# Two of the three modulation groups of each layer: issued beside the input projection, or beside the grouped-query attention

## The chip, the cores and the metric

The kernel runs on one core of one Trainium2 chip. The metric is the device time of one execution in microseconds; lower is better. Runs of one kernel scatter: the three shown below lie between 3043.15 and 3050.22 us.

## The reference

Two layers of a diffusion trunk work on 1024 sample tokens and 128 prompt tokens of width 1024. What matters here is the modulation (adaLN): two conditioning vectors, one for the sample tokens and one for the prompt tokens, go through a matrix of 1024 x 6144 in each layer, and the six rows of 1024 numbers that come out shift, scale and gate the layer's two halves.

```python
def _modulation(cvec, w, b):
    m = (jax.nn.silu(cvec) @ w + b)[:, None, :]
    return jnp.split(m, 6, axis=-1)

def _layer(x, mod, lw, ctx):
    ...
    sh1, sc1, g1, sh2, sc2, g2 = mod
    h = _rms(x, n1) * (1 + sc1) + sh1
    ...
    u_conv, qa, ka, va, qn, kn, vn = jnp.split(h @ w_in, idx, axis=-1)
    a_out = _conv_module(u_conv, dw_w, dw_b, ln_g, ln_b)
    ...
    x = x + g1 * (jnp.concatenate([a_out, b_out, c_out], axis=-1) @ w_out)
    h = _rms(x, n2) * (1 + sc2) + sh2
    x = x + g2 * (jnp.square(jax.nn.relu(h @ w1)) @ w2)
```

Here `b_out` is the grouped-query attention (6 query heads, 2 key heads, 1152 keys for a sample token) and `c_out` the neighbourhood attention. Shift and scale of the first half (`sh1`, `sc1`) are needed ahead of the projection `h @ w_in`; the other four not before the output projection `@ w_out`.

## The kernel before

The activation lies transposed in SBUF. Each layer runs through these stages: modulation group 0, first norm, convolution input, input projection, grouped-query attention, neighbourhood attention, output projection, second norm, MLP. All run on one core, and the engines' instruction streams are in program order: generators are advanced by hand, one piece at a time, and the order of these calls is the order of the instructions on every queue. A tile framework adds the semaphores.

**Modulation** (`modulation`, L183). The 6144 columns are cut into three groups of 2048: group 0 is `sh1` and `sc1`, group 1 is `g1` and `sh2`, group 2 is `sc2` and `g2`. One group runs over eight k-steps. A k-step takes four weight tiles `aw` (128 x 512, 256 KB each) and multiplies each with the two vectors `silc` into the PSUM tile `psmod` (four matmuls in the program, L224, eight records in the trace), and then issues the four DMAs for the next k-step's tiles on the SyncE queue (helper line L144). Ahead of the k-steps stands a DVE memset of `psmod` (L219); behind them a DVE copy to `mt` (L229), four transposes on TensorE into `psmt` (L233), and small DVE operations that write `mod` and one of the factors `A`. Groups 1 and 2 of a layer form one generator, `fill`. It has 23 steps: one that only fetches, and for each group a memset, eight k-steps, the copy, and the transposes with what follows them.

**Input projection** (`project`, L689). Seven column chunks (A0 to A5, then VN) by five token groups (four of two 128-token tiles, one of one tile). A token group is 24 matmuls per tile into `pst` (L541 to L543: the high and the low half of the fp32 operands in three products); then `post` takes the statistics of the heads (ACT `sq`, DVE `ss` L420), normalises (DVE `nt`, `y`, `xn`), turns the positions or applies a gain on GpSimd (L471, L484 to L490), and stores `o` to scratch in DRAM (`ddA`, `dvA`). Once per token group the convolution takes one step: DVE taps `cacc` (L102) and GpSimd taps `cacc` (L570, fed by ACT). Weights come in as `wr` and are split into `wh` (ACT) and `wl` (DVE). After every second token group (`g % 2 == 0`, three of five) the projection advances `fill` by one step: 21 of the 23 steps of a layer happen here.

**Keys.** While the last chunk VN still runs, the attention is begun: SyncE loads the keys `kd` back from `ddA`, and TensorE transposes them (`pstr` L784). This load waits for the stores of the chunks ahead of it.

**Grouped-query attention** (`gqa`, L1001, driven by `attention`, L1251). Six units of nine key tiles, with two yields per key tile, 108 ticks in all. Scores go to `psst` (L1132, L1133), the row maxima of the next unit to `psm` (L1044) and then over DVE (`mx` L1046, `nmx`) and TensorE (`psnm` L1035) into the queries, the exponentials through ACT, the products with the values to `psacc` (L1118), and the row sums through GpSimd and DVE adds `R` and TensorE (`pssum` L1084). Convolution's tail runs beside it. At each tick `attention` calls `next(fill, None)`: before the change only the last two steps of `fill` are left for it.

`aw`, `mt` and many other short-lived tiles share one ring of 18 SBUF buffers (tag T); `psmod`, `psmt`, `pst`, `psst` and the rest share eight PSUM banks.

Of the kernel before, what the change touches and what calls it, by code (L numbers as in the profile page):

```python
# [45 lines left out]
def hybrid_step(ctx, tc, I, O, depth=DEPTH):  # L46
# [104 lines left out]
    def flush(every=False):  # L151
        for x in stores:
            x[0] -= 1
        while stores and (every or stores[0][0] <= 0):
            _, out, in_ = stores.pop(0)
            load(out, in_)
# [163 lines left out]
    def run(g):  # L320
        for _ in g:
            pass
# [169 lines left out]
    def post(L, c, t, nt, ps):  # L492

        x = ps[:, 0:nt * 256].rearrange("p (t c) -> p t c", t=nt)
        o = T([nt, 256], n="o")
        lo, hi = slice(0, 128), slice(128, 256)
        normed = {"A2": hi, "A5": lo, "VN": None}.get(c, slice(0, 256))
        if normed is not None:
            st = head_stats(x[:, :, normed], nt)
        rest = {"A2": lo, "A5": hi, "VN": slice(0, 256)}.get(c)  # L500
        if rest is not None:
            acopy(o[:, :, rest], x[:, :, rest])
        yield
        if normed is not None:
            xn = head_norm(*st)
            if c in ("A0", "A1"):
                post_rope(L, c, t, nt, xn, o)
            else:
                gain(o[:, :, normed], xn, 2 if c in ("A2", "A3") else 3, nt, L)
        if t == 8:  # L510
            l, p = L.l, o[:, 0, :]
            for d, k, a, b, e in (("A1", "new_attn_k", 0, 128, 128), ("A2", "new_attn_v", 0, 0, 128), ("A4", "new_na_k", 0, 0, 256),
                                  ("A5", "new_na_k", 256, 0, 128), ("A5", "new_na_v", 0, 128, 128), ("VN", "new_na_v", 128, 0, 256)):
                if c == d:
                    store(O[k][l][:, a:a + e], p[:, b:b + e])
        if normed is not None:
            for u in range(nt):
                for d in range(2):
                    store(L.dd[c][:, t + u, :].rearrange("p (h d x) -> p h d x", d=2, x=64)[:, :, d, :],
                          o[:, u, normed].rearrange("p (h x) -> p h x", x=64))  # L520
        if rest is not None:
            store(L.dv[c][:, t:t + nt, :], o[:, :, rest])
        yield
# [10 lines left out]
    def tok_group(L, t, nt, w):  # L534
        ps = P("pst")
        for u in range(nt):
            o = ps[:, u * 256:(u + 1) * 256]
            for k in range(KT):
                hi, lo = stat(L, t + u, k)
                wh, wl = w[k]  # L540
                mm(o, hi, wh, start=(k == 0), stop=False)  # L541
                mm(o, hi, wl, start=False, stop=False)  # L542
                mm(o, lo, wh, start=False, stop=(k == KT - 1))  # L543
        return ps
# [144 lines left out]
    def project(L, pr, pre, fill):  # L689

        conv = conv_in(L, pr, pre, fill)
        next(conv)
        w = pr.weights("A0")
        for c in ORDER[2:]:
            for g, (t, nt) in enumerate(GROUPS):
                ps = tok_group(L, t, nt, w)
                if g in (1, 3):
                    pr.step()
                two = post(L, c, t, nt, ps)
                next(two)  # L700
                if conv is not None:
                    if next(conv, 0) == 0:
                        conv = None
                        L.conv = conv_all(L)
                else:
                    next(L.conv, None)
                next(two)
                if g % 2 == 0:
                    next(fill, None)
                flush()  # L710
                if c in ("A5", "VN"):
                    yield c
            if c != "VN":
                w = pr.weights(ORDER[ORDER.index(c) + 1])
            if c == "A1":
                L.tabs = None
        L.h = None
        flush(True)


    def conv_all(L):
        yield from conv_taps(L)
        l = L.l
        L.cin = None
        for si, o, n in OFFS:
            m = n // 128
            ps = P("psmu")
            for j in range(2):
                mm(ps[:, 0:n], ones, L.acc[j][:, o:o + n], start=(j == 0), stop=(j == 1))
            yield  # L730
            sqs = []
            for j in range(2):
                a = L.acc[j][:, o:o + n]
                stt(a, ps[:, 0:n], -1.0 / 256.0, a, ALU.mult, ALU.add)
                sq = T([n], n="lsq")
                act(sq, a, ACTF.Square)
                sqs.append(sq)
            yield
            tt(sqs[0], sqs[0], sqs[1], ALU.add)
            yield  # L740
            pv = P("psvr")
            mm(pv[:, 0:n], ones, sqs[0], start=True, stop=True)
            y = T([n], n="lrs")
            rsq_start(pv[:, 0:n], y, 256)
            yield
            rsq_end(pv[:, 0:n], y, sqs[1], 256)
            yield
            for j in range(2):
                a = L.acc[j][:, o:o + n]
                tt(a, a, y, ALU.mult)  # L750
            yield
            for j in range(2):
                a = L.acc[j][:, o:o + n]
                act(a, a, ACTF.Identity, scale=cvec(l, 1, j), bias=cvec(l, 2, j))
                yield
                sg = T([n], n="lsg")
                ts(sg, a, -1.0, ALU.mult, 44.0, ALU.min)
                yield
                sigmoid_end(sg)
                yield  # L760
                tt(a, a, sg, ALU.mult)
            yield

    def conv_out(L):

        yield from L.conv
        for si, o, n in OFFS:
            for j in range(2):
                a = L.acc[j][:, o:o + n]
                for chi, clo, c in c_put(si, j, 0, n):  # L770
                    acopy(chi, a[:, c])
                    yield
                    tt(clo, a[:, c], f32(chi), ALU.subtract)
                    yield
        L.acc = None
# [475 lines left out]
    def attention(L, proj, fill, op, out):  # L1251

        g = gqa(L)
        c = next(proj)
        while c:
            for _ in range(STEPS[c]):
                if L.unit < 0:
                    next(g)
            c = next(proj, None)
        while L.unit < 0:  # L1260
            next(g)
        tail = conv_out(L)
        n = natten(L)
        for i, _ in enumerate(g):
            if i % 2:
                next(tail, None)
            next(fill, None)
            if L.unit == 5 and (not L.prepared or i in (6 * 18 - 5, 6 * 18 - 2)):
                next(n)
        run(tail)  # L1270
        k = 0
        for _ in n:
            next(L.pend, None)
            next(fill, None)
            if L.step == 24:
                op.begin()
            if L.step > 25:
                for _ in range(2):
                    next(out)
        run(L.pend)  # L1280
# [513 lines left out]
    with tc.manual_schedule():  # L1794
# [4 lines left out]
        fill = modulation(0, [1, 2])  # L1799
        for l in range(depth):  # L1800
            last = l == depth - 1
            op, M = OutProj(L), Mlp(l)
            out = out_proj(L, op, M)
            attention(L, project(L, pr, pre, fill), fill, op, out)
            run(fill)
            while next(out) == "begun":
# [69 lines left out]
            fill = modulation(l + 1, [1, 2])  # L1876
# [89 lines left out]
```

## Time and profile before

| | us |
|---|---|
| median of 3 runs | 3045.22 |
| lowest, highest | 3043.15, 3050.22 |
| the profiled execution's own time | 3043.87 |
| its span in the trace | 3042.1 |
| TensorE busy over the span | 2857.0 (94%) |
| VectorE busy | 2082.6 (68%) |
| ScalarE busy | 1404.7 (46%) |
| GpSimd busy | 655.7 (22%) |
| mean granted TensorE clock | 0.97 |

The span is what the trace covers; 1.8 us of the execution lie around it. The shares are means over stages with quite different limits, so they say little of a single one. Two stages matter here, once per layer. In layer 0 the projection's first chunk starts at about 122 us and the last score maxima ahead of the attention proper end at about 348 us; the six units of the attention follow, up to about 540 us. In layer 1 the same stages begin about 1500 us later. The first k-step of `fill` in layer 0 starts at 138.9 us, and the last at 340.3 us.

### The profile page before, as it was taken

To read this page: it belongs to the slowest core of one execution; us is meant where nothing else is said; L and a number is where in the kernel's file an instruction comes from. 1 tells how busy PE (TensorE), PEld (TensorE's weight loads), DVE (VectorE), ACT (ScalarE), POOL (GpSimd) and SP (SyncE) were. 2 spreads that over 40 slices of the span, in tenths; PEclk is the share of its full clock that TensorE was granted. 3 is DMA by queue.
4 is the path that set the end of the run, shared out by engine and by line. 5 is a ranking of instruction groups with operands and counts; after the bars stand their busy time and mean duration, and the time that the engine had idled before them with its cause. 6 is when DMAs were issued, how large, how long until landed. Compare 5 with 4: busy or idle time off the path is not lost.

```text
span 3042.1 us, 52749 instructions
## 1 busy us (share of the span) xinstructions
PE 2857.0 (94%) x20328; PEld 2538.6 (83%) x20328; DVE 2082.6 (68%) x3985; ACT 1404.7 (46%) x2880; POOL 655.7 (22%) x607
## 2 busy tenths in 40 slices
PE   6998999999799998999889999999997999899999
PEld 3788645899799998999878885458997999899998
DVE  6587777855767555758665877878457765575676
ACT  4334366753544443433452353668345444334343
POOL 3576346310000000000225762553000000000000
PEclk7999999999899998999999999999998999999999
DMA  7376202433366557443433771033334653565334
GB/s 280 91 198 182 85 24 54 109 90 112 132 196 209 195 167 290 146 153 94 138 130 90 189 215 42 17 95 87 98 103 158 202 184 128 192 228 174 125 94 164
DMA packets 424124, 430.42 MB, mean 141 GB/s; under 512 B 120000, under 2 KB 299968, under 8 KB 423872
## 3 DMA queue, kind: packets, MB, share of 16 engines
q1 hardware_dynamic: 423872, 427.04, 45.1%
q8 instruction: 160, 2.62, 0.4%
q14 instruction: 92, 0.75, 0.1%
HBM read 298.50 MB, written 128.45 MB: 140 GB/s over the span
## 4 chain that ended last, share of the span: by engine, by line
PE 71%; DVE 15%; DMA 4%; ACT 4%; issue 2%; POOL 2%; SPq 1%; DVEq 0%; ACTq 0%; POOLq 0%
PE ps L1319 21%; PE psa L1319 7%; PE psc L1319 6%; PE pso L1319 5%; PE psb L1319 5%; PE psacc L1118 3%; DVE cacc L102 2%; PE pspv L985 2%; PE pspt L969 2%; PE pst L541 2%; PE pst L542 2%; PE pst L543 2%; PE psst L1132 2%; PE psd L1319 2%; PE psm L1044 2%
## 5 line engine op out<-in xcount | busy, mean ns | idle before, releaser
L1319 PE MATMUL ps<-ts,w2h 128*128 128x288 f32 x3584 | 635.9, 299 | 42.7 <-ACT w2h L96 29.1
L1319 PEld LDWEIGHTS ps<-ts,w2h 128*128 128x128 f32 x3584 | 534.3, 191 | 48.7 <-ACT w2h L96 37.2
L1319 PE MATMUL ps<-ts,w2l 128*128 128x288 f32 x1792 | 387.5, 298 | 2.0 <-DVE w2l L99 2.0
L96 ACT CAST ts<-ti 128x576 fp32r<-128x576 f32 x256 | 172.0, 672 | 328.2 <-PE ps L1319 209.1
L541 PE MATMUL pst<-wh,HA 128*128 128x256 f32 x1040 | 297.7, 286 | 0.0
L542 PE MATMUL pst<-wl,HA 128*128 128x256 f32 x1040 | 294.4, 283 | 0.1
L1319 PEld LDWEIGHTS ps<-ts,w2l 128*128 128x128 f32 x1792 | 292.2, 191 | 2.4 <-DVE w2l L99 2.2
L543 PE MATMUL pst<-wh,HA 128*128 128x256 f32 x1040 | 293.3, 282 | 0.0
L93 ACT ACTIVATE ev<-ev 128x576 f32<-128x576 f32 x224 | 153.7, 686 | 279.1 <-DVE ev L99 275.6
L99 DVE TENSOR_TENSOR ts<-ti,ts 128x576 fp32r<-128x576 f32 x256 | 195.2, 762 | 68.0 <-ACT ts L96 68.0
L102 DVE SCALAR_TENSOR_TENSOR X<-ps,mod,X 128x288 f32<-128x288 f32 x336 | 112.1, 409 | 173.5 <-PE ps L1319 173.5
L541 PEld LDWEIGHTS pst<-wh,HA 128*128 128x128 f32 x1040 | 198.1, 191 | 19.2 <-issue 6.9
L99 POOL TENSOR_TENSOR nacc<-nacc,nsq 128x512 f32<-128x512 f32 (+1 forms) x12 | 18.9, 1577 | 848.7 <-ACT nsq L93 848.7
L542 PEld LDWEIGHTS pst<-wl,HA 128*128 128x128 f32 x1040 | 198.2, 191 | 0.4 <-DVE wl L99 0.3
L543 PEld LDWEIGHTS pst<-wh,HA 128*128 128x128 f32 x1040 | 198.2, 191 | 0.0
L1755 POOL COPY yu<-X 128x128 f32<-128x128 f32 x8 | 3.9, 500 | 872.6 <-DVE X L102 872.6
L99 DVE TENSOR_TENSOR w1l<-w1r,w1h 128x512 fp32r<-128x512 f32 x128 | 87.9, 690 | 137.1 <-ACT w1h L96 136.8
L1319 PE MATMUL pso<-HA,woh 128*128 128x288 f32 x1024 | 177.8, 295 | 0.0
L1046 DVE TENSOR_REDUCE mx<-psm 128x1 f32<-128x384 f32 x288 | 142.1, 547 | 29.5 <-PE psm L1044 29.3
L1319 PE MATMUL psa<-HA,w1h 128*128 128x288 f32 x768 | 141.0, 307 | 22.0 <-ACT w1h L96 22.0
L93 ACT ACTIVATE pt<-psst 128x512 f32<-128x512 f32 x216 | 118.1, 597 | 87.7 <-PE psst L1133 86.9
L99 POOL TENSOR_TENSOR R<-R,pt 128x1024 f32<-128x1024 f32 x60 | 149.3, 2489 | 24.4 <-ACT pt L93 22.4
(275 smaller groups left out, 7065.5 us busy)
## 6 DMA issues: line engine op xcount, KB each, us to landing
ti<-hd SPq DMA_DIRECT2D x128, 576.0 KB, 3.9
hd<-ev SPq DMA_DIRECT2D x224, 288.0 KB, 3.8
aw<-in_ada_w SPq DMA_DIRECT2D x160, 256.0 KB, 3.8
w1r<-in_mlp_w SPq DMA_DIRECT2D x160, 256.0 KB, 4.4
HF<-in_mlp_w SPq DMA_DIRECT2D x128, 256.0 KB, 5.0
ddA<-o SPq DMA_DIRECT2D x144, 128.0 KB, 2.9
wr<-in_w_in SPq DMA_DIRECT2D x28, 512.0 KB, 4.0
qd<-ddA SPq DMA_DIRECT2D x48, 256.0 KB, 3.3
```

The source lines that it names most:

```text
L93: nc.scalar.activation(out=out, in_=in_, func=func, scale=scale, bias=bias, **k)
L96: nc.scalar.copy(out, in_)
L99: (eng or nc.vector).tensor_tensor(out=out, in0=a, in1=b, op=op)
L102: nc.vector.scalar_tensor_tensor(out=out, in0=a, scalar=s, in1=b, op0=op0, op1=op1)
L541: mm(o, hi, wh, start=(k == 0), stop=False)
L542: mm(o, hi, wl, start=False, stop=False)
L543: mm(o, lo, wh, start=False, stop=(k == KT - 1))
L969: nc.tensor.transpose(ps[0:n, c], self.p[j][:, o:o + n], ident)
L985: mm(ps[64 * j:64 * j + 64, 0:128], v[j], self.at[j, i], start=(i == 0), stop=(i == nb - 1))
L1046: nc.vector.tensor_reduce(out=mx[j][:, qt, b:b + 1], in_=ps[:, 0:384], op=ALU.max, axis=AX.X)
L1118: mm(acc[64 * j:64 * j + 64, :], v, pt[:, j, :], start=(kt == 0), stop=(kt == 8))
L1319: mm(ps[h][:, 0:HH], x, y[:, h * HH:(h + 1) * HH], start=(start and z == 0), stop=(stop and z == 2), skip_group_check=True)
```

## The change

Two lines go out of `project`, and the call in `attention` is made in one tick out of four:

```diff
--- before.py
+++ after.py
@@ -705,8 +705,6 @@
                 else:
                     next(L.conv, None)
                 next(two)
-                if g % 2 == 0:
-                    next(fill, None)
                 flush()
                 if c in ("A5", "VN"):
                     yield c
@@ -1264,7 +1262,8 @@
         for i, _ in enumerate(g):
             if i % 2:
                 next(tail, None)
-            next(fill, None)
+            if i % 4 == 2:
+                next(fill, None)
             if L.unit == 5 and (not L.prepared or i in (6 * 18 - 5, 6 * 18 - 2)):
                 next(n)
         run(tail)
```

All 23 steps now stand in the attention: the fetch at tick 2, the first memset at tick 6, k-steps at ticks 10 to 38, the copy at 42, transposes at 46, and so on for the second group up to tick 90. `fill` has 27 chances in 108 ticks, so it ends there.

The instruction order shows it at three places. First TensorE in the middle of the projection of layer 0, before the change; `wh` and `wl` are weight halves, `HA` halves of the normed activation:

```order
L541 MATMUL pst_1259<-wh_767,HA_74 128x256
L542 MATMUL pst_1259<-wl_768,HA_74 128x256
L543 MATMUL pst_1259<-wh_767,HA_82 128x256
L224 MATMUL psmod_1171<-aw_1010,silc 2x512
L224 MATMUL psmod_1171<-aw_1012,silc 2x512
L224 MATMUL psmod_1171<-aw_1014,silc 2x512
L224 MATMUL psmod_1171<-aw_1016,silc 2x512
L541 MATMUL pst_1317<-wh_827,HA_71 128x256
L542 MATMUL pst_1317<-wl_828,HA_71 128x256
L543 MATMUL pst_1317<-wh_827,HA_75 128x256
```

and the same place after the change:

```order
L541 MATMUL pst_1249<-wh_767,HA_74 128x256
L542 MATMUL pst_1249<-wl_768,HA_74 128x256
L543 MATMUL pst_1249<-wh_767,HA_82 128x256
L541 MATMUL pst_1295<-wh_827,HA_71 128x256
L542 MATMUL pst_1295<-wl_828,HA_71 128x256
L543 MATMUL pst_1295<-wh_827,HA_75 128x256
```

One token group's matmuls now follow the last one's directly; each of the 16 k-steps of a layer is gone from the projection in this way.

Second the SyncE queue at the end of the projection of layer 0, ahead of the first load of keys, before the change (each row is one DMA issue or a few of a kind):

```order
L144 DMA aw_2854<-in_ada_w 128x512
L144 DMA aw_2856<-in_ada_w 128x512
L144 DMA aw_2858<-in_ada_w 128x512
L144 DMA aw_2860<-in_ada_w 128x512
L144 DMA ddA_0_122<-o_2698 128x4x64 x4
L144 DMA aw_2938<-in_ada_w 128x512
L144 DMA aw_2940<-in_ada_w 128x512
L144 DMA aw_2942<-in_ada_w 128x512
L144 DMA aw_2944<-in_ada_w 128x512
L144 DMA ddA_0_122<-o_2785 128x4x64 x4
L144 DMA kd_2953<-ddA_0_119 128x9x128
```

and after it:

```order
L144 DMA ddA_0_121<-o_2362 128x4x64 x2
L144 DMA ddA_0_122<-o_2435 128x4x64 x4
L144 DMA ddA_0_122<-o_2512 128x4x64 x4
L144 DMA ddA_0_122<-o_2581 128x4x64 x4
L144 DMA ddA_0_122<-o_2656 128x4x64 x4
L144 DMA kd_2800<-ddA_0_119 128x9x128
```

The stores of the projection's results and the loads of keys keep their order; the loads of `aw` between them are gone.

Third TensorE in the first half of the attention of layer 0, after the change, at the second k-step of group 1. Before, nothing of the modulation but one `psmt` stands in the attention, and the score and value matmuls follow each other:

```order
L1131 MATMUL psst_3749<-q_3277,k_2894 128x512
L1116 MATMUL psacc_3516<-pt_3717,v_2797 64x512 x2
L1033 MATMUL psnm_3760<-ident,nmx_3753 1x128 x4
L224 MATMUL psmod_3641<-aw_3709,silc 2x512
L224 MATMUL psmod_3641<-aw_3711,silc 2x512
L224 MATMUL psmod_3641<-aw_3713,silc 2x512
L224 MATMUL psmod_3641<-aw_3715,silc 2x512
L1130 MATMUL psst_3779<-q_3208,k_2892 128x512
L1131 MATMUL psst_3779<-q_3275,k_2894 128x512
```

(Lines behind the projection are two lower after the change: L1131 is L1133 of before, L1116 is L1118.) The k-step stands between two ticks of the attention, behind one tick's products with the values and ahead of the next one's scores; the four loads for the next k-step are issued on SyncE right behind it.

## The prediction

> **What bounds the kernel now.** The page names the busiest engine first, and the chain of its section 4 runs mostly through it.
>
> ```profile
> PE 2857.0 (94%) x20328; PEld 2538.6 (83%) x20328; DVE 2082.6 (68%) x3985; ACT 1404.7 (46%) x2880; POOL 655.7 (22%) x607
> PE 71%; DVE 15%; DMA 4%; ACT 4%; issue 2%; POOL 2%; SPq 1%; DVEq 0%; ACTq 0%; POOLq 0%
> ```
>
> TensorE's 94% is a mean over the whole kernel; the change touches two stages only, so I read those in the busy time by windows: the projection up to the first load of keys (138 to 288 us), its rest (288 to 348), the attention, and the same three in layer 1.
>
> ```profile
> core 0: us, PE busy (x) PEld busy (x) DVE busy (x) ACT busy (x) POOL busy (x), PEclk, DMA share, GB/s
> 138.00:288.00 150.00, 136.84 (x1060) 119.19 (x1059) 129.41 (x158) 51.55 (x101) 113.75 (x90) 0.98 0.66 174
> 288.00:348.00 60.00, 57.19 (x445) 50.52 (x445) 37.46 (x64) 21.43 (x44) 18.59 (x11) 0.96 0.62 180
> 348.00:510.00 162.00, 152.43 (x662) 79.14 (x663) 130.22 (x218) 91.10 (x183) 84.91 (x43) 0.97 0.13 36
> 1643.00:1792.00 149.00, 137.01 (x1063) 119.57 (x1061) 129.13 (x158) 51.36 (x101) 114.75 (x90) 0.98 0.68 180
> ```
>
> The long first part of the projection is crowded on two engines: TensorE 136.8 of 150 us, VectorE 129.4, and GpSimd 113.8. Which one sets the end is told by the chain of waits cut to that window, and beside it the chain of the attention:
>
> ```profile
> by line: DVE cacc L102 18.7%; PE pst L541 9.1%; DVE nt L102 8.8%; PE pst L542 8.6%; PE pst L543 8.6%; DMA aw<-in_ada_w 8.3%; SPq L144 3.8%; POOL t L488 3.7%; DVE wl L99 3.5%; DVE y L102 3.3%; DVE ss L420 3.3%; DMA kd<-ddA 3.2%; issue 2.9%;
> by line: PE psacc L1118 20.3%; PE psst L1132 13.2%; PE psm L1044 12.0%; PE psst L1133 11.3%; DVE mx L1046 7.2%; PE psnm L1035 5.5%; DVE cacc L99 4.2%; DVE lsq L102 3.5%; PE pstr L784 2.8%; PE pssum L1084 2.5%; DVE cacc L102 2.3%; DVE lrs L1
> ```
>
> In the projection the largest item is VectorE's convolution tap, and `aw` loads are on the chain with 8.3% of 150 us, 12.5 us. The attention's chain is TensorE's. So work moves from a stage that VectorE mostly bounds to one that TensorE bounds. That is the whole case: the gain must be priced by what VectorE waits for, not by TensorE's freed time.
>
> **What goes out of the projection.** How often VectorE waits for matmuls there, layer 0 and then layer 1:
>
> ```profile
> DVE ss L420 <- ACT sq L93: 9.4, 3, 5.8
> DVE ss L420 <- ACT sq L93: 9.2, 5, 5.9
> ```
>
> `sq` is ACT's first reading of a finished `pst`, so 9.4 us is the time in which VectorE stood for a late token group. The modulation also gives VectorE work of its own:
>
> ```profile
> L229 DVE COPY mt<-psmod 128x512 f32<-128x512 f32 x1 | 0.7, 681 | 0.0
> L219 DVE MEMSET psmod<- 128x512 f32 x1 | 0.5, 485 | 0.1
> ```
>
> With both gone VectorE is earlier by 9.4 + 0.7 + 0.5 = 10.6 us in layer 0 (10.4 in layer 1); I take 10.5. The rate of `pst` matmuls, in a stretch with eight k-steps and one without any, is a second reading:
>
> ```profile
> 138.80:216.80 78.00, 58.44 (x482) 56.88 (x480) 6.01 (x11) 7.14 (x17) 1.00 0.73 200
> 216.80:262.60 45.80, 39.28 (x312) 39.01 (x312) 4.17 (x7) 3.36 (x7) 0.93 0.47 118
> ```
>
> Without k-steps a `pst` takes 45.8 / 312 = 0.147 us, so 480 would take 70.5 instead of 78.0: 7.5 us, and 9.4 if the 1.2 us of copy and memset in the second stretch are taken out. The upper bound is all that TensorE spends or waits there for the modulation:
>
> ```profile
> 138.00:288.00 150.00, 18.33 (x88) 1.89 (x88) 1.17 (x2) 0.98 0.66 174
> 288.00:348.00 60.00, 5.20 (x40) 0.53 (x40) 0.00 (x0) 0.96 0.62 180
> ...
> PE psmt L233 <- DVE mt L229: 5.7, 1, 5.7
> PE psmod L224 <- DMA aw<-in_ada_w: 5.4, 5, 1.8
> PE pstr L784 <- DMA kd<-ddA: 2.6, 1, 2.6
> ```
>
> (The first two rows count `psmod` alone.) That is 18.3 + 5.7 + 5.4 = 29.4 us up to the keys. Bounds 0 to 29.4, value 10.5, nearest to the row of VectorE's waits. What is late next is VectorE itself with its taps, then GpSimd; TensorE will stand in place of the k-steps.
>
> Behind the load of keys TensorE is dense (57.2 of 60 us), so the five k-steps there, 5.20 us or 1.04 each, are gained in full. The 2.6 us wait for `kd` stays: its stores wait for GpSimd's `o`, and the loads of `aw` lose only their queue time ahead of them. So the projection gives **10.5 + 5.2 = 15.7 us a layer**.
>
> The Trainium skill, "TensorE: Matmul & The Clock Gate", section "What's actually happening", speaks against taking filler work away: after an idle window of about 3.4 us the clock halves, and about 3.4 us of work bring it back. The trace agrees: in 240 to 262 us, behind the 5.7 us wait for `mt`, the granted clock was 0.84 in this row:
>
> ```profile
> 240.00:262.00 22.00, 18.62 (x140) 18.70 (x141) 2.50 (x4) 1.55 (x3) 0.84 0.47 115
> ```
>
> By that rule longer stands of TensorE would cost 1.7 us each as an estimate from the page; I add nothing, since that stretch ran at VectorE's pace nonetheless.
>
> **What comes into the attention.** Sixteen k-steps of 1.04 us are 16.6 us, and one more set of transposes:
>
> ```profile
> L233 PE MATMUL psmt<-ident,mt 128*128 128x128 f32 x4 | 0.7, 286 | 0.3 <-DVE mt L229 0.3
> ```
>
> 0.7 us more, 17.3. TensorE already waits in this stage, and a k-step ahead of such a wait costs less:
>
> ```profile
> PE psst L1132 <- DVE mx L1046: 2.8, 1, 2.8
> PE psnm L1035 <- DVE nmx L1029: 2.8, 2, 2.5
> PE psst L1132 <- DVE rt L99: 0.9, 2, 0.7
> PE psmu L729 <- DVE cacc L102: 0.8, 1, 0.8
> PE psvr L742 <- ACT q L96: 0.8, 1, 0.8
> PE psm L1044 <- DVE rt L99: 0.5, 1, 0.5
> PE psm L1044 <- DVE mx L1046: 0.3, 1, 0.3
> PE psmt L233 <- DVE mt L229: 0.3, 1, 0.3
> PE psm L1044 <- ACT pt L93: 0.2, 1, 0.2
> ```
>
> Together 9.4 us. The two largest end on VectorE's backlog of `mx`, which gets time to drain while TensorE does a k-step; but `mx` also needs `psm`, which a k-step delays. Bounds 0 and 9.4; I take half, 4.7. VectorE gets some 2 us more here (one copy of 0.7, two memsets of 0.5, two small writes of `mod`), of which its share of the attention's chain counts. The VectorE items shown on that line sum to 17.2%, and it is cut off; at a quarter, 0.5.
>
> The loads of `aw` must land between two steps. Four ticks lie between, and a tick follows from the row sums' groups (four unit ends, so three units of 18 ticks):
>
> ```profile
> L93 ACT ACTIVATE rr<-pssum x4: 597/597/599, 389.9 to 487.1; 128x512 f32<-128x512 f32 x4
> 271.64 1.92 SPq L144 DMA_DIRECT2D aw<-in_ada_w  x4
> DMA to landing us min/median/max: 2.8/3.7/4.9
> ```
>
> 97.2 / 54 = 1.80 us a tick, so 7.2 us, and 8.2 with the k-step itself. Issue 1.9 and landing 3.7 make 5.6, with the slowest landing 6.8, and the DMA share is 0.13 here against 0.66 in the projection. So I put no wait; the other end is 1.1 us each, the mean of the five waits above (5.4 / 5). Queued behind an unfinished k-step are `psst` of the next tick, then ACT's exponentials and VectorE's `mx`. Behind the loads on SyncE stand the next unit's query loads; a load issued late in a unit would hold them, which I price at nothing, because they are issued well ahead of their unit.
>
> The attention pays **17.3 - 4.7 + 0.5 = 13.1 us a layer**.
>
> **Sum.** 13.1 - 15.7 = -2.6 us a layer, -5.2 for two. Against the profiled execution's own 3043.87 us (span 3042.1) that is 3038.7; the median of the runs stands 1.35 us higher. I say 3039, range of this case 3031 to 3047.
>
> **Rivals.**
>
> (a) *The attention takes it nearly free.* If all 9.4 us of waits are absorbed, it pays 8.4 a layer and the result is 3043.9 - 14.6 = 3029.3; if it pays nothing, 3043.9 - 31.4 = 3012.5. For it: both large waits are VectorE's, and weight loads there fill only 79.1 of 162 us. Against it: matmul records fill 152.4 of 162, and ticks come at an even 1.80 us. About 3021, 3012 to 3031. The Trainium skill, "Perfetto Trace Analysis", section "Identifying the Most-Contended Engine", says that a TensorE's matmul busy share is no measure of its headroom and the weight loads' share is one; by that rule the attention, with 49% in that row against 79% in the projection, has the room, and the result is this rival's. The trace bears it out only so far as the waits above go.
>
> (b) *The projection gives nothing ahead of the keys* (slower). Mechanism: up to the load of keys the end is set by VectorE and GpSimd, which get in each other's way, and the time that VectorE stands for `sq` is merely moved to other waits of the same chain. Then only 5.2 us a layer is gained against 13.1: 3043.9 + 15.8 = 3060. It makes the kernel slower than before once the first part gives under 7.9 us, and measurably so (over 3051.3) under 4.2. For it: VectorE 129.4 and GpSimd 113.8 of 150. Against it: the rate of `pst`, 7.5 to 9.4. I take 3047 to 3060.
>
> (c) *The loads come late in the attention* (slower). With 1.1 us at each of 32 k-steps, 3039 + 35 = 3074; with every second one 3056. It decides once issue and landing exceed 8.2 us, by a stalled SyncE queue. For it: loads share 18 buffers with the attention's own tiles, and waited in the projection. Against it: 1.4 us to spare at the slowest landing seen.
>
> (d) *TensorE alone bounds the projection*, so that 29.4 + 5.2 = 34.6 a layer comes back instead of 15.7: 3039 - 37.8 = 3001. Against it: the stretch without k-steps, at 0.147 us a `pst` where the dense one has 0.121 (58.44 / 482).
>
> (e) *It doesn't do what it says*: `fill` is also advanced beside the neighbourhood attention, and steps could have ended there; but 27 chances are enough for 23 steps, and the order shows them. Or gain and cost cancel: 3044.
>
> **How the numbers follow.** Chances: forecast 0.45, (a) 0.18, (b) 0.14, (c) 0.10, (d) 0.07, (e) 0.06. A difference under 0.2%, 6.1 us, is about what a measurement of this kernel can't tell from no change. Faster than 3039.1 are half of the forecast, (a) and (d): 0.47; slower than 3051.3 are most of (c) and two thirds of (b): 0.19, say 0.20; the rest, 0.33, is between. The range leaves out (d) and half of (c), with the tips of (a) and (b): 3014 to 3058.
>
> **What would show it.** In the profile after: VectorE's wait for `sq` ahead of the keys nearly gone, TensorE's waits there on VectorE instead; the load of keys about 10 us earlier in each layer, the first scores of the attention about 16 us earlier; the attention about 13 us longer, its waits on `mx` and `nmx` about halved, and hardly any wait of `psmod` for `aw`. Load of keys not earlier: (b). Waits of `psmod` for `aw` over 0.4 us each in the attention: (c). Attention longer by under 9 us: (a). TensorE dense ahead of the keys: (d).

## The result, and the profile after

| | before | after |
|---|---|---|
| median, us | 3044.18 (4 runs, 3042.25 to 3050.22) | 3072.02 (4 runs, 3069.54 to 3072.82) |
| profiled execution, us | 3043.87 | 3071.43 |
| span in the trace, us | 3042.1 | 3069.6 |

The ratio is 1.0086, with a 95% interval of 1.0074 to 1.0098: the change costs 0.9%, and the range of the prediction ended at 3058. The forecast was wrong in sign.

The first reading is the busy time by windows, now cut at the events of each trace: from about 25 us behind the first `pst` of the projection to the first transpose of keys, from there to the first score, and from the first to the last score of the attention, for layer 0 and layer 1. (The first `pst` of layer 0 stands at 107.4 us before the change; the 122 us named further up lie within the projection's first chunk.) First before:

```profile
core 0: us, PE busy (x) PEld busy (x) DVE busy (x) ACT busy (x) POOL busy (x), PEclk, DMA share, GB/s
133.00:288.50 155.50, 141.84 (x1103) 124.21 (x1102) 134.50 (x165) 52.53 (x103) 115.64 (x91) 0.98 0.65 172
288.50:348.00 59.50, 57.19 (x445) 50.50 (x445) 36.96 (x64) 21.43 (x44) 18.09 (x11) 0.96 0.62 180
348.00:537.30 189.30, 177.66 (x789) 92.89 (x789) 148.06 (x252) 110.34 (x232) 104.84 (x56) 0.98 0.12 32
1638.50:1792.30 153.80, 141.51 (x1102) 124.07 (x1101) 133.59 (x165) 52.34 (x103) 116.01 (x91) 0.98 0.68 179
1792.30:1850.20 57.90, 55.55 (x444) 48.75 (x444) 38.50 (x65) 22.38 (x45) 18.73 (x11) 0.99 0.64 184
1850.20:2039.40 189.20, 177.55 (x789) 93.21 (x789) 148.08 (x252) 110.45 (x232) 104.82 (x56) 0.98 0.12 32
```

and the same stages after:

```profile
132.00:282.00 150.00, 124.33 (x1015) 123.22 (x1014) 133.43 (x160) 52.16 (x103) 118.31 (x91) 0.92 0.44 103
282.00:337.50 55.50, 53.17 (x404) 50.90 (x404) 37.23 (x64) 21.46 (x44) 18.64 (x11) 0.93 0.45 127
337.50:550.20 212.70, 195.02 (x922) 94.51 (x921) 151.28 (x257) 110.65 (x232) 103.68 (x56) 0.98 0.34 105
1651.00:1799.00 148.00, 124.69 (x1012) 123.41 (x1012) 136.44 (x160) 51.78 (x103) 121.05 (x91) 0.93 0.46 108
1799.00:1853.50 54.50, 52.20 (x405) 49.91 (x405) 38.62 (x65) 22.37 (x45) 19.16 (x11) 0.95 0.46 129
1853.50:2071.40 217.90, 200.34 (x922) 97.77 (x921) 152.19 (x257) 111.03 (x232) 103.50 (x56) 0.95 0.34 102
```

With the exact starts of the first `pst`, the first transpose of keys and the scores, the 27.5 us of the span split so:

| stage | layer 0 | layer 1 | forecast for each |
|---|---|---|---|
| first `pst` to keys | 181.1 to 175.1: -6.0 | 179.5 to 173.4: -6.1 | -10.5 |
| keys to first score | 59.4 to 55.5: -3.9 | 57.9 to 54.5: -3.4 | -5.2 |
| first to last score | 189.4 to 212.6: +23.2 | 189.2 to 217.9: +28.7 | +13.1 |

The rest (-0.7 up to the first `pst` of layer 1, -4.4 behind the attention of layer 1) was not followed further. So the projection gave about two thirds of what was forecast, and the attention took about twice as much. The rows split the attention's loss in two. In layer 0 TensorE was busy 17.4 us longer (195.0 against 177.7, at the same granted clock of 0.98) and idle 6.1 us longer (17.7 against 11.6). In layer 1 its idle time grew as much (17.6 against 11.7), but its busy time by 22.8 us, at a clock of 0.95 against 0.98.

In the projection VectorE's wait for `sq` is gone as forecast. In its place stands another one. The waits of VectorE ahead of the keys of layer 0, and ACT's:

```profile
DVE wl L99 <- ACT wh L96: 6.5, 2, 5.3
...
DVE ss L420 <- ACT sq L93: 0.3, 1, 0.3
ACT wh L96 <- POOL cacc L570: 5.0, 1, 5.0
```

ACT's cast `wh` stood 5.0 us for GpSimd's tap (`wh` and the tap's operand take turns in one ring of buffers), and VectorE's `wl` stood for `wh`. Layer 1 doesn't have this wait on ACT; there the same 30 taps of VectorE took longer, first before, then after:

```profile
L102 DVE SCALAR_TENSOR_TENSOR cacc<-cin,vecs,cacc 128x1167 f32<-128x1167 f32 x30 | 53.0, 1768 | 0.5
L102 DVE SCALAR_TENSOR_TENSOR cacc<-cin,vecs,cacc 128x1167 f32<-128x1167 f32 x30 | 59.0, 1965 | 0.5
```

All of VectorE's work in that window grew from 133.6 to 136.4 us, though the copy and the memset had left it. At the end of this part TensorE stands for the keys until 282 us and then works at half clock; the second row is the window from 276 to 288 us, with the clock behind TensorE's busy time:

```profile
PE pstr L782 <- DMA kd<-ddA: 13.2, 1, 13.2
276.00:288.00 12.00, 5.97 (x29) 0.50 0.98 261
```

In the attention of layer 0 the waits of TensorE after the change are these:

```profile
PE psnm L1033 <- DVE nmx L1027: 5.0, 3, 2.5
PE psmu L727 <- DVE cacc L102: 4.0, 1, 4.0
PE psst L1130 <- DVE mx L1044: 2.9, 1, 2.9
PE psnm L1033 <- DVE mx L1044: 2.7, 2, 1.7
PE pstr L782 <- DVE k L99: 1.5, 1, 1.5
PE pspt L967 <- ACT pp L93: 0.6, 1, 0.6
PE psm L1042 <- DVE rt L99: 0.5, 1, 0.5
PE psm L1042 <- ACT pt L93: 0.2, 1, 0.2
```

They sum to 17.4 us, against 11.4 before over the same stage. None is for `aw`: the loads were in time. All the large ones are for VectorE, and they grew where the forecast had halved them.

### The profile page after: what moved, and what is told of

Same layout as the page of the kernel before. It is cut to its first block, busy times and chain, and to the rows that moved or that the text cites. A ratio compares the mean times of both kernels' runs of the same rounds, so it can differ in the third digit from the quotient of the medians.

```text
span 3069.6 us, 52782 instructions
## 1 busy us (share of the span) xinstructions
PE 2851.9 (93%) x20328; PEld 2543.3 (83%) x20328; DVE 2090.2 (68%) x3985; ACT 1403.6 (46%) x2880; POOL 662.6 (22%) x607
## 4 chain that ended last, share of the span: by engine, by line
PE 71%; DVE 18%; ACT 4%; DMA 3%; issue 2%; POOL 1%; SPq 1%; DVEq 0%; ACTq 0%; POOLq 0%
PE ps L1318 21%; PE psa L1318 7%; PE psc L1318 6%; PE pso L1318 5%; PE psb L1318 5%; DVE cacc L102 4%; PE psacc L1116 3%; PE pspv L983 2%; PE pspt L967 2%; DVE nt L102 2%; PE psst L1130 2%; PE psd L1318 2%; PE psmod L224 1%; PE pst L542 1%; PE pst L541 1%
## 5 line engine op out<-in xcount | busy, mean ns | idle before, releaser
L541 PEld LDWEIGHTS pst<-wh,HA 128*128 128x128 f32 x1040 | 201.3, 194 | 14.6 <-ACT wh L96 14.0
L543 PEld LDWEIGHTS pst<-wh,HA 128*128 128x128 f32 x1040 | 201.5, 194 | 0.0
L99 DVE TENSOR_TENSOR w1l<-w1r,w1h 128x512 fp32r<-128x512 f32 x128 | 87.8, 689 | 136.4 <-ACT w1h L96 133.1
```

What stands on the lines that cost most here:

```text
L99: (eng or nc.vector).tensor_tensor(out=out, in0=a, in1=b, op=op)
```

## The experiments

Twelve kernels. `psmu` is the first matmul of the convolution's tail; it needs the last taps `cacc`. The last two of VectorE's taps stand in the tail themselves, ahead of it.

| run | edit | median, us | ratio to before (95%) |
|---|---|---|---|
| e1_block | changed, all steps in a block behind the attention | 3149.24 (one run) | |
| e2_quarter | changed, a quarter of each k-step's matmuls | 3068.94 | 1.0081 (1.0060 to 1.0103) |
| f1_onestep | changed, one k-step of eight | 3035.8 | 0.9968 (0.9957 to 0.9980) |
| e4_phase3 | changed, step one tick later | 3061.91 | 1.0052 (1.0036 to 1.0069) |
| f2_latetail | changed, tail from tick 9 | 3045.56 | 1.0004 (0.9994 to 1.0014) |
| g3_phase3_latetail | both | 3043.58 | 0.9987 (0.9977 to 0.9996) |
| g1_before_latetail | before, tail from tick 9 | 3046.92 | 1.0007 (0.9997 to 1.0017) |
| h1_nopooltaps | changed, without GpSimd's taps | 3012.93 (one run) | |
| e5_a2a5 | before, steps in chunks A2 to A5 | 3059.6 | 1.0048 (1.0030 to 1.0066) |
| f3_prefetch2 | before, loads two steps ahead | 3057.91 | 1.0041 (1.0027 to 1.0055) |
| f4_nojoint | steps ahead of the keys, without stops for VectorE | 3030.29 | 0.9950 (0.9936 to 0.9965) |
| g2_nojoint_latetail | f4 and tail from tick 9 | 3031.11 | 0.9950 (0.9938 to 0.9963) |

**e1_block: both stages without the modulation.**

```diff
-            if i % 4 == 2:
-                next(fill, None)
...
         run(tail)
+        run(fill)
```

> All 23 modulation steps of a layer are run in one block between the two attentions, so projection and grouped-query attention are both free of them. Theory A (the projection is set by VectorE and GpSimd; what TensorE gains beyond them is handed back in the attention's first unit as waits on cacc and nmx): first transposes of keys 6 to 7 us earlier than before in layer 0, first scores about 10 earlier, and the attention 3 to 5 us LONGER than before (189.3) though it holds no k-step. Theory B (the waits in the attention come from the k-steps themselves): attention 189 or less, gain of about 10 kept to its end. The block itself is exposed: 16 times about 6.7 us (issue 1.9, landing 3.7, matmuls 1.0), so about 100 us a layer, total about 3220.

The stages in this trace, from keys at 284.2 us in layer 0 (175.4 behind its first `pst`, as in the changed kernel): the attention took 194.3 us in layer 0 and 194.2 in layer 1, 4.9 and 5.0 longer than before, with no k-step in it. That is theory A's figure. The block cost less than expected, about 55 us a layer.

```profile
339.60:533.90 194.30, 180.34 (x786) 94.67 (x785) 148.16 (x247) 110.55 (x232) 104.45 (x56) 0.95 0.12 34
...
PE psmu L727 <- DVE cacc L102: 3.9, 1, 3.9
```

The window row is the attention of layer 0: TensorE is busy 180.3 us for the same matmuls that took 177.7 before, at a granted clock of 0.95 against 0.98, and idle 14.0 against 11.6. So 2.3 of the 5 us are waits and 2.7 are slower matmuls. The wait for `cacc` is 3.9 against 0.8. f4_nojoint, described below, has no k-step in its attention either:

```profile
337.80:528.60 190.80, 176.93 (x786) 92.26 (x785) 145.96 (x247) 110.29 (x232) 104.87 (x56) 0.97 0.12 32
PE psmu L745 <- DVE cacc L102: 4.2, 1, 4.2
```

Its wait for `cacc` is as long and its idle time the same (13.9 us), but at a clock of 0.97 the stage takes only 1.4 us longer than before. The other part of e1_block's 5 us therefore goes with the clock; why that was lower in both layers of e1_block isn't known.

What VectorE and GpSimd did at the wait, in the timeline (start, us, engine), e1_block first, and then before:

```profile
344.69 6.47 DVE L102 SCALAR_TENSOR_TENSOR cacc<-cin,vecs,cacc 128x1167 f32<-128x1167 f32 x2
344.08 2.42 POOL L99 TENSOR_TENSOR R<-pt,pt 128x1024 f32<-128x1024 f32 x1 [31.01 <-ACT pt L93]
346.86 3.07 POOL L99 TENSOR_TENSOR R<-R,pt 128x1024 f32<-128x1024 f32 x1 [0.35 <-ACT pt L93]
...
353.94 3.85 DVE L102 SCALAR_TENSOR_TENSOR cacc<-cin,vecs,cacc 128x1167 f32<-128x1167 f32 x2
352.74 2.37 POOL L99 TENSOR_TENSOR R<-pt,pt 128x1024 f32<-128x1024 f32 x1 [34.14 <-ACT pt L93]
356.49 3.52 POOL L99 TENSOR_TENSOR R<-R,pt 128x1024 f32<-128x1024 f32 x1 [1.39 <-ACT pt L93]
```

Taken one by one, the two taps took 3.04 and 3.39 us in e1_block, 2.38 and 1.43 before. The first begins while GpSimd's first add runs, in both. The second begins 0.9 us after the second add in e1_block, and 0.1 us ahead of it before the change. f3_prefetch2, a variant of the kernel before that is described below, has both orders, one in each layer (second tap and second add, layer 0 and then layer 1):

```profile
359.12 1.43 DVE L102 SCALAR_TENSOR_TENSOR cacc<-cin,vecs,cacc 128x1167 f32<-128x1167 f32 x1
359.20 3.57 POOL L99 TENSOR_TENSOR R<-R,pt 128x1024 f32<-128x1024 f32 x1 [1.34 <-ACT pt L93]
1870.57 3.50 DVE L102 SCALAR_TENSOR_TENSOR cacc<-cin,vecs,cacc 128x1167 f32<-128x1167 f32 x1
1870.51 2.34 POOL L99 TENSOR_TENSOR R<-R,pt 128x1024 f32<-128x1024 f32 x1 [1.20 <-ACT pt L93]
```

`psmu` waits 0.9 us in its layer 0 and 3.1 in its layer 1. So the longer wait for `cacc` is no backlog brought along from the projection, as theory A had it, but two operations that meet here, and about 0.1 us decides which of them comes first. Before the change VectorE's copy `mt` (0.67 us) stood shortly ahead of the taps in its queue; f3_prefetch2 has it in both layers, so the copy alone doesn't settle the order. h1_nopooltaps, below, has the same wait.

**e2_quarter and f1_onestep: what a k-step costs.** The first drops three of the four matmuls of every k-step, the second all four of seven k-steps in eight. (Both also cut the later modulation group 0 of layer 1, which runs beside the MLP, so I read them by stage.)

```diff
-                for j in range(4):
+                for j in range(4 if first else 1):                        # e2_quarter
+                for j in range(4 if first or k == 0 else 0):              # f1_onestep
```

> As the changed kernel, but a k-step does only the first of its four matmuls (the modulation's other three quarters of groups 1 and 2 are left out); loads, copies, memsets and transposes stay. If TensorE's own time in the attention is the price (theory B): 16 x 0.78 us = 12.5 a layer less, so about 3047. If loads, the PSUM bank that psmod holds, or VectorE's work are the price: over 3062. If the waits also go with the matmuls: under 3043.

> As the changed kernel, but of a group's eight k-steps only the first does its matmuls (7 of 8 are left out: the modulation groups 1 and 2 then hold an eighth of the sum); loads of aw, copies, memsets and transposes stay at their places. A k-step of one matmul took as long as one of four, so this run takes the whole step away. If TensorE's time for the steps is the price of the attention: 14 x 1.06 = 14.8 us less a layer, attention about 198, time about 3042. If loads or the bank held by psmod are the price: over 3060.

e2_quarter changed the attention of layer 0 from 212.6 to 214.9 us (the granted clock from 0.98 to 0.96) and that of layer 1 from 217.9 to 212.8 (from 0.95 to 0.98), with the idle time as it was. Taken alone this speaks for another price than TensorE's. The timeline says why it doesn't: a k-step in this kernel, the score behind it, and the same two in the changed kernel.

```profile
481.93 1.02 PE L224 MATMUL psmod<-aw,silc 128*2 128x512 f32 x2
482.88 0.50 PE L1130 MATMUL psst<-q,k 128*128 128x512 f32 x1
...
481.54 1.04 PE L224 MATMUL psmod<-aw,silc 128*2 128x512 f32 x8
482.51 0.50 PE L1130 MATMUL psst<-q,k 128*128 128x512 f32 x1
```

One matmul (two records) holds TensorE for 0.95 us up to the next start, four hold it for 0.97: they run side by side. The run had taken nothing away. f1_onestep takes whole steps away, and the attention falls from 212.6 to 198.8 in layer 0 and from 217.9 to 202.4 in layer 1: 13.8 and 15.5 us for 14 steps, 0.99 and 1.1 each. So the steps were paid in full. With e1_block the 23.2 us of layer 0 split into 4.9 with no step there, 4.5 more for two steps, the memsets, the copies and the transposes, the loads and the bank that `psmod` holds, and 13.8 for the other fourteen.

```profile
337.10:536.00 198.90, 180.95 (x810) 93.66 (x809) 151.12 (x257) 110.72 (x232) 103.61 (x56) 0.98 0.37 112
```

This row, the attention of layer 0 in f1_onestep, says something more: without those fourteen steps TensorE is busy 14.1 us less than after the change and idle just as long (17.9 us against 17.7). On balance the steps neither filled TensorE's waits nor lengthened them. What lengthened them is still in the kernel when those steps are gone.

**e4_phase3, f2_latetail, g3_phase3_latetail, g1_before_latetail: steps and tail.** The step one tick later, or the tail, with the last two taps in it, four calls later:

```diff
-            if i % 4 == 2:
+            if i % 4 == 3:                 # e4_phase3, g3_phase3_latetail
...
-            if i % 2:
+            if i % 2 and i > 8:            # f2, g1, g2, g3
                 next(tail, None)
```

> As the changed kernel, but the step stands at ticks 3, 7, 11 ... (behind the second half of a key tile) in place of 2, 6, 10. If the place inside a tick matters for the waits on mx and nmx, up to 6 us a layer either way (3060 to 3084); if TensorE's time is the whole price, 3072 within 4.

> As the changed kernel, but the convolution's tail (whose first matmul psmu waits for the last taps cacc on VectorE) begins at tick 9 of the attention instead of tick 1. If the wait of 4 us for cacc and the slow clock behind it hand back what the projection gained (theory A): 4 to 8 us a layer less, 3056 to 3064. If the wait only moves to another instruction (nmx, mx): 3070 or more.

> The changed kernel with both edits: step at ticks 3, 7, 11 ... and tail from tick 9. If both gains are the same one (the steps of the first unit running into the tail): 3040 to 3046. If they add: about 3035.

> The kernel before with the convolution's tail beginning at tick 9 of the attention. If the early tail hurts only where the attention starts ahead of VectorE's taps (as in the changed kernel): 3038 to 3045, since TensorE waits only 0.8 us for cacc here. If the early tail is a loss in itself: 10 us a layer as in f2_latetail, about 3024.

Both edits help the changed kernel. The late tail gives 26.5 us, where 8 to 16 were expected, the later step 10.1; together they give 3043.6, only 2.0 less than the late tail alone, so most of the later step's gain is contained in the other. On the kernel before, the late tail gives nothing. TensorE in the attention's first three units, after the change and then in f2_latetail:

```profile
337.50:378.30 40.80, 32.66 (x140) 0.94 0.20 62
378.30:414.90 36.60, 36.41 (x183) 1.00 0.50 161
414.90:452.50 37.60, 33.03 (x143) 0.95 0.15 48
...
337.70:368.80 31.10, 31.10 (x138) 0.92 0.25 79
368.80:409.90 41.10, 37.62 (x181) 0.96 0.47 148
409.90:444.20 34.30, 32.51 (x146) 1.00 0.17 50
```

(Columns: window, its length, TensorE busy, granted clock, DMA share, GB/s.) In the first unit 8.1 us of idle time become none, in the second 0.2 become 3.5, in the third 4.6 become 1.8. The idle time of TensorE over the whole attention (length less busy time, us) in the runs that tell steps and tail apart:

| run | layer 0 | layer 1 |
|---|---|---|
| before | 11.6 | 11.7 |
| e1_block (no step) | 14.0 | 13.5 |
| f1_onestep (two steps) | 17.9 | 19.0 |
| changed | 17.7 | 17.6 |
| e4_phase3 | 13.6 | 12.0 |
| f2_latetail | 8.2 | 8.3 |
| g1_before_latetail (no step) | 11.2 | 10.9 |

With the late tail, then, the steps do absorb waits: 3.4 us of those before the change, 3.0 of those in g1_before_latetail. The attention of layer 0 pays 12.9 us, close to the 13.1 forecast; with the tail where it was, waits grew by 6.1. Of the 26.5 us that the late tail gives, 18.8 are idle time of the two attentions; most of the rest is TensorE's busy time in layer 1 (193.0 us at a clock of 0.98, against 200.3 at 0.95). So the growth of the idle time needs both, the modulation's pieces and the tail early in the attention. How they hinder each other isn't shown: in the changed kernel the steps stand at even ticks and the tail at odd ones, and e4_phase3, which puts them into the same ticks, is the faster.

**h1_nopooltaps: is GpSimd the pace of the projection?** Taps 1 to 21 of one channel half, which GpSimd adds, are left out, with ACT's products for them.

```diff
-                p = S([CW], n="cp")
-                act(p, cin[:, k:k + CW], ACTF.Copy, scale=dww(L.l, j, k))
-                nc.gpsimd.tensor_tensor(out=acc[:, 0:CW], in0=acc[:, 0:CW], in1=p, op=ALU.add)
+                pass
```

> The changed kernel without the convolution taps that GpSimd adds (taps 1 to 21 of the second channel half are left out, ACT's products for them too); VectorE's own taps and all else stay. If VectorE's slower operations beside GpSimd, and ACT's casts that wait for GpSimd's taps, are what took 4 of the 10.5 us that the projection should have gained: VectorE's 30 taps ahead of the keys fall from about 56 us to under 50, the 5 us wait of wl for wh goes, and the keys come at least 8 us earlier than in the changed kernel (first transposes before 274 us in layer 0). If VectorE's own work sets the pace: at most 3 us earlier.

From the first `pst` to the keys this kernel takes 144.4 us in layer 0 and 148.2 in layer 1, where the changed one takes 175.1 and 173.4: 31 and 25 us less. VectorE's taps fall from 56.2 to 49.2 us in layer 0, and the wait of `wl` is gone. The third row is one of the small operations of VectorE; after the change it took 14.7 us, 611 ns for one:

```profile
L102 DVE SCALAR_TENSOR_TENSOR cacc<-cin,vecs,cacc 128x1167 f32<-128x1167 f32 x30 | 49.2, 1639 | 0.5
L99 DVE TENSOR_TENSOR wl<-wr,wh 128x1024 fp32r<-128x1024 f32 x10 | 14.3, 1431 | 0.1
L102 DVE SCALAR_TENSOR_TENSOR y<-nt,y 128x8 f32<-128x8 f32 (+2 forms) x24 | 5.5, 229 | 0.8
```

So GpSimd's taps (with ACT's products for them, which this run can't tell apart) set VectorE's pace there. The large taps are the smaller part of it: they fall by 7.0 us, but the three small operations `y` and `nt` of 128 x 8, 24 of each, fall from 38.5 us together to 18.6. In this kernel VectorE waits for matmuls again ahead of the keys, 7.4 us for `sq`, which speaks against a backlog; and still the last two taps take 6.38 us beside GpSimd's adds and `psmu` waits 3.8 us. That wait belongs to the attention's start.

**e5_a2a5, f3_prefetch2, f4_nojoint, g2_nojoint_latetail: can the projection take the steps more cheaply?**

```diff
-                if g % 2 == 0:
+                if c in ("A2", "A3", "A4", "A5"):          # e5_a2a5
+                if g != 3 and c not in ("VN",):            # f4_nojoint, g2_nojoint_latetail
                     next(fill, None)
...
-        for _ in range(6 if first else 1):
+        for _ in range(6 if first else 2):                 # f3_prefetch2
             fetch()
...
             mt = T([512], n="mt")                          # f4_nojoint, g2_nojoint_latetail
             nc.vector.tensor_copy(mt, ps)
+            open_ = r, mt
+            if n + 1 < len(groups):
+                ps = cleared()
             yield
```

In f4_nojoint the transposes of a group (`finish`) follow at the next group's second k-step, or one empty step behind the last copy.

> The kernel before, but the steps stand in chunks A2 to A5 at every token group (20) instead of every second group of all seven chunks; the last three fall into the attention's first ticks. Theory A: in A0 and A1 TensorE sets the pace and a k-step costs its own time, from A3 on VectorE does and a k-step is free: kept gain of 5 to 10 us a layer against before, 3025 to 3035. If loads of aw at every group come late and stop TensorE there: 3044 or more.

> The kernel before, with the weight tiles of the modulation fetched two k-steps ahead instead of one. If the late loads of aw (5.4 us of waits in layer 0) are what made VectorE stand for sq: 4 to 8 us a layer less, 3028 to 3036. If VectorE and GpSimd together are the bound, as the changed kernel's keys (6.5 earlier instead of 10.5) suggest, and other tiles of the ring come later: 3038 to 3050.

> The kernel before, with all 22 steps of the modulation ahead of the load of keys (chunks A0 to A5, four token groups of five), the second psmod cleared with the first one's copy, and the transposes of a group one or two steps behind its copy, so that TensorE doesn't stop for VectorE's memset (9.5 us in e5_a2a5) or copy. Theory A: keys as in the changed kernel or up to 3 us later, none of the 5.2 us behind them, attention free of k-steps: 3030 to 3040. If k-steps delay VectorE there whatever their place: 3045 to 3060.

> f4_nojoint with the tail beginning at tick 9. There TensorE waits 4.2 us for cacc again, so the gain of the late tail should come on top: 5 to 10 us a layer less than f4's 3030, so 3010 to 3022. If the wait moves to mx or nmx: 3026 to 3032.

The first two are slower than before. f3_prefetch2 lies outside both cases of its expectation; e5_a2a5 has the time of its second case, but not the cause. Their waits of TensorE in the projection of layer 0, e5_a2a5 and then f3_prefetch2:

```profile
PE psmod L224 <- DVE psmod L219: 9.5, 1, 9.5
...
PE psmt L233 <- DVE mt L229: 13.1, 1, 13.1
PE psmod L224 <- DMA aw<-in_ada_w: 0.5, 1, 0.5
```

It isn't the loads: two steps ahead they were in time (0.5 us), and the kernel lost 13.6. TensorE stood 13.1 us at the transposes for a copy that waited in VectorE's queue, and in e5_a2a5 9.5 us for the memset, 3.6 for a copy and 2.6 for loads. But the kernel before had stops there too, 5.7 us for the copy and 5.4 for the loads. So the stops together grew by 4.6 us in e5_a2a5 and 2.5 in f3_prefetch2, and the keys of layer 0 come 1.3 and 2.4 us later behind the first `pst` (in layer 1 2.1 and 3.6). Most of the loss stands in the attention: 197.2 and 196.4 us in e5_a2a5, where the last k-step, the copy and the transposes are left for it and `psmt` waits 4.6 us for `mt`, at a clock of 0.95; and 189.5 and 196.3 in f3_prefetch2, at 0.98 and 0.94.

f4_nojoint takes out these two joints and puts all steps ahead of the keys, and is 0.50% faster than before (interval 0.35% to 0.64%): its keys come 179.5 us behind the first `pst` in both layers, 1.6 us earlier than before in layer 0 and as before in layer 1, with more steps ahead of them; the stretch behind them takes 51.9 and 53.3 us instead of 59.4 and 57.9, and the attention 190.8 and 190.2. So its gain is made behind the keys, where five k-steps are gone. It changes the joints and the places at once; no run has the one without the other, so what the joints are worth isn't shown. The late tail adds nothing there: in the attention of layer 0 TensorE's idle time falls from 13.9 to 10.8 us, but its busy time grows from 176.9 to 179.5. The time is that of the expectation's second case, though the waits shrank and didn't only move.

## Why the prediction was wrong

- **Which engine bounds which stage: right.** VectorE's wait for `sq` went from 9.4 to 0.3 us, and TensorE stood for VectorE instead.
- **10.5 us ahead of the keys: the size was wrong, 6.0 and 6.1.** The term took all of VectorE's waits as gain. GpSimd, "then GpSimd" in the list of what is late next, was next at once: its tap held ACT's cast for 5.0 us in layer 0, and in layer 1 VectorE's own taps took 6.0 us longer beside it. This is part of rival (b)'s mechanism. The Trainium skill, "SBUF — State Buffer", section "Who interferes with whom", says that VectorE and GpSimd share a pair of ports, and that a VectorE instruction with two SBUF inputs contends with a GpSimd one that reads. The trace agrees: two taps, which read two tiles in SBUF each, took 6.47 us where each began while an add of GpSimd ran, and 3.85 where one of them began first. The prediction had the taps in its chain line and didn't ask what their time depended on.
- **5.2 us behind the keys: 3.9 and 3.4.** TensorE now waits 13.2 us for the keys in layer 0 (2.6 before) and begins the stretch at half clock; over the stretch it is 0.93 instead of 0.96. Over 55.5 and 59.5 us these clocks cost 3.9 and 2.4 us of full speed, as an estimate from the rows; that is 1.5 more than before, near the 1.3 that are missing (in layer 1 2.1 and 1.8). The prediction named such a cost of longer stands and set it to nothing.
- **17.3 us for the steps in the attention: right.** TensorE's busy time grew by 17.4 us in layer 0, and f1_onestep gives 0.99 us for each step.
- **4.7 us absorbed: wrong, and this is the step that failed most.** TensorE's idle time grew by 6.1 us instead. The prediction took the waits of before, for VectorE's `mx` and `nmx` above all, as slack that inserted work could fill. f1_onestep shows that fourteen of the sixteen steps filled nothing on balance: the idle time is the same without them. Of the 6.1 us, 2.3 come with no step at all (e1_block), and the other 3.8 with what f1_onestep still holds: the first steps, VectorE's memsets, copies and small writes, the transposes and the loads. Which of these it is stays open. f2_latetail shows that the absorption would have come true, with 3.4 us, had the convolution's tail begun later.
- **Not in the sum: the attention's start without any step.** e1_block's attention is 5 us longer than before, 2.3 of it idle time (counted above) and 2.7 a lower clock that f4_nojoint, 1.4 us longer in all, doesn't have. The 0.8 us wait for `cacc` in the prediction's list was the place: it is 0.8 us or 3 to 4, by which of a tap and a GpSimd add begins first.
- **Layer 1.** The attention there took 5 us more than in layer 0, with the same idle time, at a granted clock of 0.95 against 0.98. What sets the clock apart between two equal stages isn't settled.
- **Loads in time: right.** `psmod` waited for no `aw` in the attention; rival (c) didn't happen. Rival (a), by the weight loads' share, would have needed the steps to be nearly free; they cost their full time, so here TensorE's matmul share told more of its room than the weight loads' share.

What stays open: which tick-by-tick order makes the modulation's pieces and the tail collide. The runs show that moving the tail removes nearly all of the loss (26.5 of 27.8 us) and moving the step about a third of it, not the rule by which to place them.

## What to carry to other kernels

Don't count an engine's waits as room for inserted work until a run has shown it: here with the convolution's tail early fourteen inserted steps filled none of them, and with the tail late the steps filled 3 us. When work leaves a stage that three engines share, price the gain by the third engine too, and look for instructions whose duration differs from one place to another, since these will change. And split the time of a stage into busy and idle time with the granted clock beside it before you name a cause: here the same attention in two layers differed by 5 us at equal idle time. A stop counts by what it adds to the stops it replaces.

## What the runs showed of the hardware

Four matmuls with a 128 x 2 stationary tile each, written to four different groups of 32 output partitions, held TensorE for 0.97 us, one alone for 0.95 us. In f1_onestep's attention fourteen such steps came to 0.99 us each.

A VectorE tap of 128 x 1167 (two inputs in SBUF) that began while a GpSimd add of 128 x 1024 ran ended 1.2 us after that add, by the profile's times of both: before the change at 356.3 us after 355.1, in e1_block at 347.7 after 346.5 and at 351.2 after 349.9. One that began first, by 0.1 us, took 1.43 us, and then the add took 3.52 or 3.57 us; adds that began with no tap running took 2.4. An operation of 128 x 8 met the same:

```profile
357.92 2.11 DVE L102 SCALAR_TENSOR_TENSOR A<-mod,vecs 128x8 f32<-128x8 f32 x1
```

It began, in the kernel before, while the add of 3.52 us ran, and ended with it, at 360.0 us.

In the window that holds the end of TensorE's wait of 13.2 us and the 6 us of work behind it the granted clock was 0.50; in the next 12 us it was 1.00.
